# Decay tables of a gated recurrent mixer: one running sum over 128 tokens and more exponentials, in place of 16-token sums and doubling

## The chip, the cores and the metric

One core of one Trainium2 chip. The metric is device time in microseconds (us) for one execution of the whole kernel. The engines are named as the profile names them: PE is TensorE (PEld its weight loads), DVE VectorE, ACT ScalarE, POOL GpSimd, and SP issues transfers.

## The reference

A bidirectional encoder of two layers on 1024 tokens of width 1024. Layer 0 mixes with windowed attention, layer 1 with a gated linear recurrence in both directions; each also has four cross-attention heads and ends with a convolutional feed-forward. The change lies in the recurrence, one head of which is (8 heads, keys and values 128 wide, in each direction):

```python
f = lb + (1.0 - lb) * sigmoid(z)          # forget gate, per key channel
log_f, k = log(f), 1.0 - f
b = cumsum(log_f, axis=2)                 # within a chunk
q_dec = q * exp(b)
k_dec = k * exp(-b)
k_end = k * exp(b_end - b)
s = where(causal, q_dec @ k_dec.T, 0)     # o_intra = s @ v
...
o = q_dec @ state
state = exp(b_end) * state + k_end.T @ v
```

The chunk length is free: the same result follows from any cut of the tokens. What has to be right is that no exponential overflows, since `exp(-b)` grows with the length over which `b` is summed.

## The kernel before

Matrix products run on PE as three products of split operands (a high part `wh`, `uh` and a rest `wl`, `ul`): `mm3`, lines 80 to 82. ACT makes the high part (`wunit`, a cast, line 75), DVE the rest (line 76).

The mixer is `hgrn()`. `proj(h)` projects for a head: `proj_fm` makes q and the two gates' inputs with channels on the partitions, 512 tokens at a time, into one of two PSUM banks `pj`; its exponentials go to `q` and to `s`. Every second head, `proj_tm` makes v and the output gate of two heads, for 8 tiles of 128 tokens, two tiles in turn in the two `pj` banks. A bank of it is read by DVE (copy to `v`, line 1113), by ACT (first of the three activations of `sigmoid`, line 1091; the other two, lines 1092 and 1093, work on `gs`) and by DVE again (product, line 1115). There are four such passes, in what the page shows as about 1262 to 1310, 1424 to 1470, 1588 to 1634 and 1752 to 1799 us.

`direction(h, r, d, b, ...)` is called 32 times (8 heads, 2 directions, 2 halves of 512 tokens). Within a chunk of 128 tokens it builds the products of queries and keys `pa` in blocks: 32x32 blocks on the diagonal (from E2 and E1), and one level each of 32 and of 64 tokens below it (from G). Their factors need decays relative to a point near the block. Before, the sum `B` starts anew every 16 tokens (`smask`), `R` is the rest to the end of the 16, `EP` and `ER` are their exponentials, and `step(n)` doubles the length that EP and ER cover by multiplying one half of each with the other's end value (lines 1217, 1218), until they cover 128 and serve `qin`, `dec` and the keys for the state. Then four transposes of ER (line 1256), its copy `kT`, the products `pu` (line 1261), and the state's steps `S` on DVE (line 1270). `output` sums what meets the queries and normalizes it (`po`, lines 1285 and 1292; squares on line 99).

`early` is the pool of the tables: five buffers E, two EP and two ER, 2 KB each a partition. A scheduler sets the order in which each engine's queue holds its instructions, from dependencies, buffers, priorities and its own estimates; on the chip each engine runs its queue in that order. `tc.high_priority(AHEAD)` raises the instructions inside it, here the handling of the banks and the `pa` products.

Of the kernel before, what the change touches and what calls it, by code (L numbers as in the profile page):

```python
# [46 lines left out]
def build(tc, A, out):  # L47
# [983 lines left out]
    def hgrn():  # L1031
# [28 lines left out]
        nc.sync.dma_start(bng, A["b_norm_g"])  # L1060
        gm = [one([P, 512], f"gm{d}", U8) for d in range(2)]
        for d in range(2):
            gf = early.tile([P, 512], F32, tag="E", bufs=5, name="gf")
            nc.sync.dma_start(gf, A["gmask"][d])
            dve.tensor_copy(gm[d], gf)
        smask = one([P, 512], "smask", BF16)
        pool.memset(smask, 1.0)
        pool.memset(smask.rearrange("p (b c) -> p b c", c=16)[:, :, 0:1], 0.0)
        lmx = one([P, 2, 8], "lmx")
        dve.tensor_tensor(lmx, lg[:, :, 0, :], lg[:, :, 1, :], op=ALU.max)  # L1070
        dve.tensor_tensor(lg, lg, bc(lmx.unsqueeze(2), [P, 2, 2, 8]), op=ALU.subtract)
# [90 lines left out]
        def direction(h, r, d, b, qin, S, As):  # L1162

            q, k = r["q"][b], r["s"][d][b]
            rev = slice(None, None, -1) if d else slice(None)
            lt, er = (0, 1) if d else (1, 0)

            def E():
                return early.tile([P, 512], F32, tag="E", bufs=5, name="E")

            def halves(x, n):
                x = x.rearrange("p (b a c) -> p b a c", a=2, c=n)
                return x[:, :, lt, :], x[:, :, er, :]


            a_ = E()
            act.activation(k, k, AF.Ln, bias=1.0)
            act.activation(k, k, AF.Exp, scale=-1.0)
            act.activation(a_, k, AF.Ln, bias=lb[:, d, h:h + 1], scale=oml[:, d, h:h + 1])
            act.activation(k, k, AF.Identity, bias=oml[:, d, h:h + 1], scale=noml[:, d, h:h + 1])  # L1180
            R, B = E(), E()
            dve.tensor_tensor_scan(B[:, rev], smask, a_[:, rev], 0.0, op0=ALU.mult, op1=ALU.add)
            v16 = lambda x: x.rearrange("p (b c) -> p b c", c=16)
            e = 0 if d else 15
            dve.tensor_tensor(v16(R), bc(v16(B)[:, :, e:e + 1], [P, 32, 16]), v16(B), op=ALU.subtract)

            EP = early.tile([P, 512], F32, tag="EP", bufs=2, name="EP")
            ER = early.tile([P, 512], F32, tag="ER", bufs=2, name="ER")
            act.activation(EP, B, AF.Exp)
            act.activation(ER, R, AF.Exp)  # L1190
            pa = PA[d]
            E1, E2 = E(), E()
            Bl, Be = halves(B, 16)
            Rl, Re = halves(R, 16)
            l1, e1 = halves(E1, 16)
            l2, e2 = halves(E2, 16)

            def parts(n):
                return halves(EP, n) + halves(ER, n) + halves(q, n) + halves(k, n)

            pl_, pe_, rl_, re_, ql, qe, kl, ke = parts(16)
            act.activation(e1, Re, AF.Exp, scale=-1.0)
            act.activation(l2, Bl, AF.Exp, scale=-1.0)
            dve.tensor_tensor(l1, pl_, ql, op=ALU.mult)
            dve.tensor_tensor(e2, re_, ke, op=ALU.mult)
            dve.tensor_tensor(e1, e1, qe, op=ALU.mult)
            dve.tensor_tensor(l2, l2, kl, op=ALU.mult)
            def block(c, i, j, x, y, n=32):

                return pe.matmul(pa[i:i + 32, c, j:j + n], x[:, c * P + i:c * P + i + 32], y[:, c * P + j:c * P + j + n],  # L1210
                                 start=True, stop=True, tile_position=(0, i))

            def step(n):
                pl_, pe_, rl_, re_ = parts(n)[:4]
                e = 0 if d else n - 1
                nb = 512 // (2 * n)
                dve.tensor_tensor(re_, re_, bc(pl_[:, :, e:e + 1], [P, nb, n]), op=ALU.mult)
                dve.tensor_tensor(pl_, pl_, bc(pe_[:, :, e:e + 1], [P, nb, n]), op=ALU.mult)

            for n in (32, 64):  # L1220
                step(n // 2)
                G = E()
                gl, ge = halves(G, n)
                pl_, pe_, rl_, re_, ql, qe, kl, ke = parts(n)
                pool.tensor_tensor(gl, pl_, ql, op=ALU.mult)
                dve.tensor_tensor(ge, re_, ke, op=ALU.mult)
                if n == 32:
                    G32 = G
            with tc.high_priority(AHEAD):
                for c in range(4):  # L1230
                    for o in (0, 32):
                        mm = block(c, er * 64 + o, lt * 64, G, G, 64)
                with tc.issue_after(mm.ins):
                    for c in range(4):
                        for o in range(0, P, 32):
                            block(c, o, o, E2, E1)
                    for c in range(4):
                        for o in (0, 64):
                            block(c, o + er * 32, o + lt * 32, G32, G32)
            step(64)  # L1240
            dec = wp.tile([P, 4], F32, tag="dec", bufs=2, name="dec")
            e = 0 if d else P - 1
            pool.tensor_copy(dec.unsqueeze(2), EP.rearrange("p (c t) -> p c t", t=P)[:, :, e:e + 1])
            bs = slice(b * 512, (b + 1) * 512)
            sum_steps[1].send(pool.tensor_tensor(qin[:, bs], EP, q, op=ALU.mult))
            dve.tensor_tensor(ER, ER, k, op=ALU.mult)
            dve.copy_predicated(Az[d], gm[d], pa.rearrange("p c t -> p (c t)"))
            a2 = lambda x: x.rearrange("p c t -> p (c t)")
            if As[b] is None:
                As[b] = wp.tile([P, 4, P], F32, tag="As", bufs=2, name="As")  # L1250
                act.copy(a2(As[b]), Az[d])
            else:
                pool.tensor_tensor(a2(As[b]), a2(As[b]), Az[d], op=ALU.add)
            tp = bank("pt")
            for c in range(4):
                pe.transpose(tp[:, c, :], ER[:, c * P:(c + 1) * P], ident)
            kT = wp.tile([P, 4, P], F32, tag="kT", bufs=1, name="kT")
            act.copy(kT, tp)
            pu = bank("pu")
            for c in range(4):  # L1260
                pe.matmul(pu[:, c, :], kT[:, c, :], r["v"][:, 4 * b + c, :], start=True, stop=True)
            for c in (range(3, -1, -1) if d else range(4)):
                cg = 4 * b + c
                nx = cg - 1 if d else cg + 1
                if not 0 <= nx < NT:
                    continue
                if cg == (NT - 1 if d else 0):
                    act.copy(S[:, nx, :], pu[:, c, :])
                else:
                    dve.scalar_tensor_tensor(S[:, nx, :], S[:, cg, :], dec[:, c:c + 1], pu[:, c, :],  # L1270
                                             op0=ALU.mult, op1=ALU.add)
# [300 lines left out]
```

## Time and profile before

| | |
|---|---|
| median of 3 runs | 2664.08 us (2660.1 to 2664.66) |
| the profiled execution | 2660.75 us, span 2658.9 us |
| PE busy | 2605.2 us, 98% of the span |
| DVE, ACT, POOL busy | 67%, 53%, 18% |
| granted clock of PE | 0.997 |
| the mixer's stretch, 1227.6 to 1900 us | PE 662.5, DVE 476.1, ACT 377.4, POOL 179.2 of 672.4 us |

A group's row in the profile reads: line, engine, operation, written tile <- read tiles, shapes, count, then busy time in us and mean ns of one, then the idle time of the engine in front of these instructions and what ended it. The tile names are the program's; `E` stands for any of the E buffers, `s` for what the code calls `k` in `direction`.

### The profile page before, as it was taken

What the parts mean: (1) busy time and instruction counts of PE and PEld (TensorE: products, weight loads), DVE (VectorE), ACT (ScalarE), POOL (GpSimd) and SP (SyncE); (2) the same over time, 40 slices, a digit from 0 to 9 for tenths busy, and PEclk for the clock granted to TensorE, in tenths of its full rate; (3) what the DMA queues carried; (4) which work ended last, traced back from release to release, by engine and by line L of the source; (5) the groups of instructions that cost most, each with busy time, mean ns of one, the idle gap of its engine ahead of it and who ended that gap; (6) DMA issues with size and microseconds to landing.
All of it is one profiled execution on the core that took longest, in us unless ns stands there. A gap on an engine that the chain in (4) does not pass through costs nothing. (4 is left out here: it accounts for less than half of the span.)

```text
span 2658.9 us, 39054 instructions
## 1 busy us (share of the span) xinstructions
PE 2605.2 (98%) x14420; PEld 2185.9 (82%) x14420; DVE 1771.2 (67%) x2948; ACT 1399.1 (53%) x2534; POOL 472.2 (18%) x520
## 2 busy tenths in 40 slices
PE   8999999999999999999999999999999999999998
PEld 7888887788888888887888878888887788888887
DVE  6678886578555565477677675876757755656447
ACT  6467676545444445455464554656534444445453
POOL 0321010211111100032234131231211111110013
PEclk9999999999999999999999999999999999999999
DMA  9782222367777756674236251103336778785666
GB/s 353 243 176 58 74 86 83 101 193 194 198 201 195 206 154 221 215 265 151 84 112 167 66 124 54 53 25 113 127 105 195 194 193 209 198 202 170 205 207 236
DMA packets 195727, 425.92 MB, mean 160 GB/s; under 512 B 20048, under 2 KB 56272, under 8 KB 189904
## 3 DMA queue, kind: packets, MB, share of 16 engines
q1 hardware_dynamic: 161552, 324.06, 37.6%
q0 software_dynamic: 24544, 90.19, 16.3%
q10 hardware_dynamic: 9440, 9.19, 1.0%
q8 instruction: 113, 1.85, 0.3%
q14 instruction: 78, 0.64, 0.1%
HBM read 330.04 MB, written 116.39 MB: 168 GB/s over the span
## 5 line engine op out<-in xcount | busy, mean ns | idle before, releaser
L86 DVE TENSOR_TENSOR wl<-st,wh 128x1024 fp32r<-128x1024 f32 (+1 forms) x238 | 261.4, 1105 | 316.8 <-ACT wh L85 294.1
L85 ACT CAST wh<-st 128x1024 fp32r<-128x1024 f32 (+1 forms) x238 | 222.4, 937 | 288.7 <-PE X L574 186.5
L80 PE MATMUL pj<-uh,wh 128*128 128x512 f32 x512 | 203.6, 398 | 2.2 <-DVE q L1129 0.8
L574 PE MATMUL X<-wl,wh 128*128 128x512 f32 x528 | 205.0, 390 | 0.3 <-DVE wl L86 0.3
L574 PE MATMUL X<-wh,wl 128*128 128x512 f32 x528 | 204.9, 389 | 0.0
L81 PE MATMUL pj<-ul,wh 128*128 128x512 f32 x512 | 202.4, 395 | 0.0
L82 PE MATMUL pj<-uh,wl 128*128 128x512 f32 x512 | 202.3, 395 | 0.0
L574 PE MATMUL X<-wh 128*128 128x512 f32 x528 | 198.6, 390 | 0.0
L80 PE MATMUL pj<-wh,uh 128*128 128x384 f32 (+1 forms) x512 | 189.4, 372 | 5.0 <-DVE gs L1115 2.6
L82 PE MATMUL pj<-wh,ul 128*128 128x384 f32 (+1 forms) x512 | 187.7, 367 | 0.0
L81 PE MATMUL pj<-wl,uh 128*128 128x384 f32 (+1 forms) x512 | 187.2, 366 | 0.0
L76 DVE TENSOR_TENSOR wl<-st,wh 128x1024 fp32r<-128x1024 f32 (+1 forms) x91 | 113.9, 1256 | 30.9 <-ACT wh L75 29.8
L574 PE MATMUL V<-uh,wh 128*128 128x512 f32 x336 | 130.7, 389 | 0.0
L574 PE MATMUL V<-ul,wh 128*128 128x512 f32 x336 | 130.7, 389 | 0.0
L574 PE MATMUL V<-uh,wl 128*128 128x512 f32 x336 | 130.7, 389 | 0.0
L75 ACT CAST wh<-st 128x1024 fp32r<-128x1024 f32 (+1 forms) x97 | 97.8, 1014 | 37.5 <-PE pj L81 16.4
L574 PEld LDWEIGHTS X<-wl,wh 128*128 128x128 f32 x528 | 99.1, 188 | 21.6 <-DVE wl L86 1.2
L574 PEld LDWEIGHTS X<-wh,wl 128*128 128x128 f32 x528 | 99.1, 188 | 20.7
L574 PEld LDWEIGHTS X<-wh 128*128 128x128 f32 x528 | 99.1, 188 | 20.5
L80 PEld LDWEIGHTS pj<-uh,wh 128*128 128x128 f32 x512 | 96.5, 189 | 21.7 <-DVE q L1129 1.2
L82 PEld LDWEIGHTS pj<-uh,wl 128*128 128x128 f32 x512 | 96.5, 189 | 19.0
L81 PEld LDWEIGHTS pj<-ul,wh 128*128 128x128 f32 x512 | 96.5, 188 | 18.6 <-DVE ul L86 0.4
(411 smaller groups left out, 7149.2 us busy)
## 6 DMA issues: line engine op xcount, KB each, us to landing
st<-hid SPq DMA_DIRECT2D x154, 256.0 KB, 3.4
st<-in_ffw_dram SPq DMA_DIRECT2D x108, 256.0 KB, 3.7
w2s<-in_ffw_dram POOLq DMA_DIRECT2D x24, 1024.0 KB, 8.0
st<-in_ffw_dram SPq DMA_DIRECT2D x46, 512.0 KB, 4.3
hid<-tt SPq DMA_DIRECT2D x88, 256.0 KB, 4.7
st<-w2s SPq DMA_DIRECT2D x88, 256.0 KB, 3.2
sx<-in_ffw_dram SPq DMA_DIRECT2D x84, 256.0 KB, 3.9
sy<-in_ffw_dram SPq DMA_DIRECT2D x42, 512.0 KB, 6.4
```

Source lines behind the costliest of these rows:

```text
L75: act.copy(h[:, :n], raw)
L76: (eng or dve).tensor_tensor(l[:, :n], raw, h[:, :n].bitcast(F32), op=ALU.subtract)
L80: pe.matmul(o, ah, bh, start=first, stop=False)
L81: pe.matmul(o, ah, bl, start=False, stop=False)
L82: return pe.matmul(o, al, bh, start=False, stop=last)
L85: act.copy(h, src)
L86: dve.tensor_tensor(l, src, h.bitcast(F32), op=ALU.subtract)
L574: last = pe.matmul(o, x, y, start=new, stop=e, skip_group_check=not first)
```

## The change

`B` is now one sum over each chunk of 128 tokens (`smask` is zero at every 128th). For blocks of length 2n, `from_middle(n)` subtracts from B its own value at the block's middle, for n = 16, 32 and 64, each on all 512 columns on DVE. E1 and E2 are exponentials of that difference with plus and minus sign on all columns; the level factors G are exponentials of half of the columns each, written in place, and multiplied by q on POOL and by k on DVE as before. EP is one exponential of B; ER four exponentials, one for each chunk of 128, with the chunk's end value as the bias. R and the doubling steps are gone. Buffers: four E, two D (which also holds the logarithm), one B, one EP, one ER; nine in all, as before.

```diff
--- before.py
+++ after.py
@@ -1060,12 +1060,12 @@
         nc.sync.dma_start(bng, A["b_norm_g"])
         gm = [one([P, 512], f"gm{d}", U8) for d in range(2)]
         for d in range(2):
-            gf = early.tile([P, 512], F32, tag="E", bufs=5, name="gf")
+            gf = early.tile([P, 512], F32, tag="E", bufs=4, name="gf")
             nc.sync.dma_start(gf, A["gmask"][d])
             dve.tensor_copy(gm[d], gf)
         smask = one([P, 512], "smask", BF16)
         pool.memset(smask, 1.0)
-        pool.memset(smask.rearrange("p (b c) -> p b c", c=16)[:, :, 0:1], 0.0)
+        pool.memset(smask.rearrange("p (b c) -> p b c", c=P)[:, :, 0:1], 0.0)
         lmx = one([P, 2, 8], "lmx")
         dve.tensor_tensor(lmx, lg[:, :, 0, :], lg[:, :, 1, :], op=ALU.max)
         dve.tensor_tensor(lg, lg, bc(lmx.unsqueeze(2), [P, 2, 2, 8]), op=ALU.subtract)
@@ -1165,79 +1165,67 @@
             rev = slice(None, None, -1) if d else slice(None)
             lt, er = (0, 1) if d else (1, 0)
 
-            def E():
-                return early.tile([P, 512], F32, tag="E", bufs=5, name="E")
+            def E(tag="E", bufs=4):
+                return early.tile([P, 512], F32, tag=tag, bufs=bufs, name=tag)
 
             def halves(x, n):
                 x = x.rearrange("p (b a c) -> p b a c", a=2, c=n)
                 return x[:, :, lt, :], x[:, :, er, :]
 
-
-            a_ = E()
             act.activation(k, k, AF.Ln, bias=1.0)
             act.activation(k, k, AF.Exp, scale=-1.0)
+            a_ = E("D", 2)
             act.activation(a_, k, AF.Ln, bias=lb[:, d, h:h + 1], scale=oml[:, d, h:h + 1])
             act.activation(k, k, AF.Identity, bias=oml[:, d, h:h + 1], scale=noml[:, d, h:h + 1])
-            R, B = E(), E()
+            B = E("B", 1)
             dve.tensor_tensor_scan(B[:, rev], smask, a_[:, rev], 0.0, op0=ALU.mult, op1=ALU.add)
-            v16 = lambda x: x.rearrange("p (b c) -> p b c", c=16)
-            e = 0 if d else 15
-            dve.tensor_tensor(v16(R), bc(v16(B)[:, :, e:e + 1], [P, 32, 16]), v16(B), op=ALU.subtract)
-
-            EP = early.tile([P, 512], F32, tag="EP", bufs=2, name="EP")
-            ER = early.tile([P, 512], F32, tag="ER", bufs=2, name="ER")
-            act.activation(EP, B, AF.Exp)
-            act.activation(ER, R, AF.Exp)
+
+            def from_middle(n):
+
+                D = E("D", 2)
+                v = lambda x: x.rearrange("p (b c) -> p b c", c=2 * n)
+                m = n if d else n - 1
+                dve.tensor_tensor(v(D), v(B), bc(v(B)[:, :, m:m + 1], [P, 512 // (2 * n), 2 * n]), op=ALU.subtract)
+                return D
+
+            D = from_middle(16)
+            E1, E2 = E(), E()
+            act.activation(E1, D, AF.Exp)
+            act.activation(E2, D, AF.Exp, scale=-1.0)
+            dve.tensor_tensor(E1, E1, q, op=ALU.mult)
+            dve.tensor_tensor(E2, E2, k, op=ALU.mult)
             pa = PA[d]
-            E1, E2 = E(), E()
-            Bl, Be = halves(B, 16)
-            Rl, Re = halves(R, 16)
-            l1, e1 = halves(E1, 16)
-            l2, e2 = halves(E2, 16)
-
-            def parts(n):
-                return halves(EP, n) + halves(ER, n) + halves(q, n) + halves(k, n)
-
-            pl_, pe_, rl_, re_, ql, qe, kl, ke = parts(16)
-            act.activation(e1, Re, AF.Exp, scale=-1.0)
-            act.activation(l2, Bl, AF.Exp, scale=-1.0)
-            dve.tensor_tensor(l1, pl_, ql, op=ALU.mult)
-            dve.tensor_tensor(e2, re_, ke, op=ALU.mult)
-            dve.tensor_tensor(e1, e1, qe, op=ALU.mult)
-            dve.tensor_tensor(l2, l2, kl, op=ALU.mult)
             def block(c, i, j, x, y, n=32):
 
                 return pe.matmul(pa[i:i + 32, c, j:j + n], x[:, c * P + i:c * P + i + 32], y[:, c * P + j:c * P + j + n],
                                  start=True, stop=True, tile_position=(0, i))
 
-            def step(n):
-                pl_, pe_, rl_, re_ = parts(n)[:4]
-                e = 0 if d else n - 1
-                nb = 512 // (2 * n)
-                dve.tensor_tensor(re_, re_, bc(pl_[:, :, e:e + 1], [P, nb, n]), op=ALU.mult)
-                dve.tensor_tensor(pl_, pl_, bc(pe_[:, :, e:e + 1], [P, nb, n]), op=ALU.mult)
-
+            G = {}
             for n in (32, 64):
-                step(n // 2)
-                G = E()
-                gl, ge = halves(G, n)
-                pl_, pe_, rl_, re_, ql, qe, kl, ke = parts(n)
-                pool.tensor_tensor(gl, pl_, ql, op=ALU.mult)
-                dve.tensor_tensor(ge, re_, ke, op=ALU.mult)
-                if n == 32:
-                    G32 = G
+                D = from_middle(n)
+                G[n] = E()
+                (dl, de), (gl, ge), (ql, _), (_, ke) = (halves(x, n) for x in (D, G[n], q, k))
+                act.activation(gl, dl, AF.Exp)
+                act.activation(ge, de, AF.Exp, scale=-1.0)
+                pool.tensor_tensor(gl, gl, ql, op=ALU.mult)
+                dve.tensor_tensor(ge, ge, ke, op=ALU.mult)
             with tc.high_priority(AHEAD):
                 for c in range(4):
                     for o in (0, 32):
-                        mm = block(c, er * 64 + o, lt * 64, G, G, 64)
+                        mm = block(c, er * 64 + o, lt * 64, G[64], G[64], 64)
                 with tc.issue_after(mm.ins):
                     for c in range(4):
                         for o in range(0, P, 32):
                             block(c, o, o, E2, E1)
                     for c in range(4):
                         for o in (0, 64):
-                            block(c, o + er * 32, o + lt * 32, G32, G32)
-            step(64)
+                            block(c, o + er * 32, o + lt * 32, G[32], G[32])
+            EP, ER = E("EP", 1), E("ER", 1)
+            act.activation(EP, B, AF.Exp)
+            for c in range(4):
+                x = slice(c * P, (c + 1) * P)
+                m = c * P + (0 if d else P - 1)
+                act.activation(ER[:, x], B[:, x], AF.Exp, bias=B[:, m:m + 1], scale=-1.0)
             dec = wp.tile([P, 4], F32, tag="dec", bufs=2, name="dec")
             e = 0 if d else P - 1
             pool.tensor_copy(dec.unsqueeze(2), EP.rearrange("p (c t) -> p c t", t=P)[:, :, e:e + 1])
```

The set of PE's instructions is the same, and so are SP's transfers. What stands in the queues is not. The first place is ACT's queue in the third pass of `proj_tm`, where the banks of v and gate of the second and third tile are handled. Before:

```order
L1091 ACTIVATE gs<-pj 128x2x128
L1092 ACTIVATE gs<-gs 128x2x128
L1093 ACTIVATE gs<-gs 128x2x128
L1258 COPY kT<-pt 128x512
L1091 ACTIVATE gs<-pj 128x2x128
L1190 ACTIVATE ER<-E 128x512
L1092 ACTIVATE gs<-gs 128x2x128
L1093 ACTIVATE gs<-gs 128x2x128
L1179 ACTIVATE E<-s,lb,oml 128x512
L1180 ACTIVATE s<-s,oml,noml 128x512
L1091 ACTIVATE gs<-pj 128x2x128
L1092 ACTIVATE gs<-gs 128x2x128
```

After, from the third tile on (line numbers have moved below the change: 1178 and 1179 are the former 1179 and 1180, 1208 and 1209 the new exponentials of G, 1228 the pieces of ER):

```order
L1091 ACTIVATE gs<-pj 128x2x128
L1228 ACTIVATE ER<-B 128x128 x2
L1178 ACTIVATE D<-s,lb,oml 128x512
L1092 ACTIVATE gs<-gs 128x2x128
L1208 ACTIVATE E<-D 128x4x64
L1209 ACTIVATE E<-D 128x4x64
L1179 ACTIVATE s<-s,oml,noml 128x512
L1093 ACTIVATE gs<-gs 128x2x128
L1091 ACTIVATE gs<-pj 128x2x128
L1228 ACTIVATE ER<-B 128x128 x4
L1092 ACTIVATE gs<-gs 128x2x128
L1193 ACTIVATE E<-D 128x512
```

Between the first and the third activation of a tile's gate stood one exponential or nothing; now six others stand there in the third tile (two pieces of ER count as two), and eight in the fourth, of which the list shows the first four.

The second place is PE's queue in the same pass, at the end of the second pair of tiles. Before, a block of `pa` in the midst of a tile, and then transposes and products:

```order
L82 MATMUL pj<-wh,ul 128x512
L1261 MATMUL pu<-v,kT 128x128 x2
L1256 MATMUL pt<-ident,ER 128x128 x4
L80 MATMUL pj<-wh,uh 128x512
L81 MATMUL pj<-wl,uh 128x512
L1210 MATMUL pa<-E 32x64 x8
L1210 MATMUL pa<-E 32x32 x24
L82 MATMUL pj<-wh,ul 128x512
```

After, with the products of the states and the transposes of ER ahead of the block, all between two tiles:

```order
L82 MATMUL pj<-wh,ul 128x512
L1249 MATMUL pu<-v,kT 128x128
L1244 MATMUL pt<-ident,ER 128x128 x4
L1200 MATMUL pa<-E 32x64 x8
L1200 MATMUL pa<-E 32x32 x24
L80 MATMUL pj<-wh,uh 128x512
L81 MATMUL pj<-wl,uh 128x512
L82 MATMUL pj<-wh,ul 128x512
```

The block and the transposes have moved to the boundary where PE next needs a bank back.

The third place is DVE's queue in the first call of `direction`. Before:

```order
L1182 SCALAR_TENSOR_TENSOR E<-smask,E 128x512
L1185 TENSOR_TENSOR E<-E 128x512
L1204 TENSOR_TENSOR E<-EP,q 128x16x16
L1205 TENSOR_TENSOR E<-ER,s 128x16x16
L1206 TENSOR_TENSOR E<-E,q 128x16x16
L1217 TENSOR_TENSOR ER<-ER,EP 128x16x16
L1207 TENSOR_TENSOR E<-E,s 128x16x16
L1218 TENSOR_TENSOR EP<-EP 128x16x16
L1226 TENSOR_TENSOR E<-ER,s 128x8x32
```

After:

```order
L1181 SCALAR_TENSOR_TENSOR B<-smask,D 128x512
L1188 TENSOR_TENSOR D<-B 128x512 x2
L1234 TENSOR_TENSOR ER<-ER,s 128x512
L1195 TENSOR_TENSOR E<-E,q 128x512
L1196 TENSOR_TENSOR E<-E,s 128x512
L1188 TENSOR_TENSOR D<-B 128x512
L1211 TENSOR_TENSOR E<-E,s 128x8x32
```

The doubling steps and the half-width products have left, the differences and full-width products stand there, and the product for the state (`ER<-ER,s`) has moved ahead of those for `pa`.

## The prediction

> **What bounds the kernel now.** I read the page first, for the busy shares, then the stage of the change in a table of windows, then TensorE's waits in that stage, then the groups of instructions that the change touches, and last the timeline of one handover.
>
> ```profile
> span 2658.9 us, 39054 instructions
> ...
> PE 2605.2 (98%) x14420; PEld 2185.9 (82%) x14420; DVE 1771.2 (67%) x2948; ACT 1399.1 (53%) x2534; POOL 472.2 (18%) x520
> ```
>
> ```profile
> 1227.60:1900.00 672.40, 662.54 (x5233) 557.43 (x5233) 476.09 (x941) 377.37 (x801) 179.15 (x189) 1.00 0.31 90
> ```
>
> The second fence is the recurrent mixer alone (columns: window, length, busy time and count of PE, weight loads, DVE, ACT, POOL, then clock, DMA share, GB/s). TensorE is busy 662.5 of 672.4 us at full clock. The change leaves its instructions as they are, so they give nothing back; at most the 9.9 us of idle time can be won. DVE is at 71% there, ACT at 56%, POOL at 27%. So the question is which waits TensorE has now, and which it gets. In the same stretch it waits for:
>
> ```profile
> PE pj L80 <- DVE gs L1115: 2.6, 3, 1.2
> PE pu L1261 <- DVE S L1270: 2.5, 2, 1.7
> PE pt L1256 <- ACT ot L1315: 2.3, 2, 2.1
> PE pj L80 <- DVE q L1129: 0.8, 1, 0.8
> PE po L1285 <- DVE S L1270: 0.6, 1, 0.6
> ```
>
> (total, times, longest). No row names `pa`, the product that the decay tables feed: TensorE never waits for the tables, and a shorter way to them wins nothing by itself. The largest wait is another: in the four passes that project v and the gate, TensorE fills two banks in turn, and a bank is free again only after DVE's copy of v, three activations of the gate on ACT, and DVE's product. The timeline of one such handover:
>
> ```profile
> 1455.63 0.39 PE L82 MATMUL pj<-wh,ul 128*128 128x512 f32 x1
> 1455.86 0.39 PE L80 MATMUL pj<-wh,uh 128*128 128x512 f32 x1
> ...
> 1458.58 0.39 PE L80 MATMUL pj<-wh,uh 128*128 128x512 f32 x1
> ```
>
> ```profile
> 1456.06 0.43 DVE L1113 COPY v<-pj 128x256 f32<-128x256 f32 x1 [4.10 <-PE pj L82]
> 1457.84 0.42 DVE L1115 TENSOR_TENSOR gs<-pj,gs 128x256 f32<-128x256 f32 x1 [1.35 <-ACT gs L1093]
> ```
>
> ```profile
> 1456.52 0.38 ACT L1091 ACTIVATE gs<-pj 128x256 f32<-128x256 f32 x1 [5.02 <-DVE v L1113]
> 1456.94 0.42 ACT L1092 ACTIVATE gs<-gs 128x256 f32<-128x256 f32 x1
> 1457.39 0.42 ACT L1093 ACTIVATE gs<-gs 128x256 f32<-128x256 f32 x1
> ```
>
> The bank is complete at 1456.02 (1455.63 + 0.39) and free at 1458.26, 2.2 us later. Meanwhile TensorE runs the last twelve matmuls of the other bank, from 1455.86 on, and at 1458.58 it starts on the first bank again. The slack is 0.3 us. Whatever else ACT does between the first and the third of these activations beyond 0.3 us is paid by TensorE, unless it has other work there.
>
> **The change, part by part.** Durations are means in the stage:
>
> ```profile
> L1217 DVE TENSOR_TENSOR ER<-ER,EP 128x256 f32<-128x256 f32 x96 | 57.1, 595 | 2.1
> L1218 DVE TENSOR_TENSOR EP<-EP 128x256 f32<-128x256 f32 x96 | 44.2, 460 | 5.8 <-POOL E L1225 1.9
> L1246 DVE TENSOR_TENSOR ER<-ER,s 128x512 f32<-128x512 f32 x32 | 22.8, 714 | 0.1
> L1185 DVE TENSOR_TENSOR E<-E 128x512 f32<-128x512 f32 x32 | 21.9, 685 | 1.2
> L1205 DVE TENSOR_TENSOR E<-ER,s 128x256 f32<-128x256 f32 x32 | 20.6, 643 | 7.8 <-ACT ER L1190 7.4
> L1204 DVE TENSOR_TENSOR E<-EP,q 128x256 f32<-128x256 f32 x32 | 18.5, 579 | 0.2 <-ACT EP L1189 0.2
> L1206 DVE TENSOR_TENSOR E<-E,q 128x256 f32<-128x256 f32 x32 | 14.5, 452 | 1.7 <-ACT E L1202 1.7
> L1207 DVE TENSOR_TENSOR E<-E,s 128x256 f32<-128x256 f32 x32 | 13.3, 417 | 0.0
> ```
>
> DVE, for each of the 32 calls of `direction`: out go the subtraction for R (0.69), three doubling steps (3 x 1.06 = 3.17) and four half-width products (2.09), 5.94 us; in come three differences at R's price (2.06) and two full-width products at L1246's (1.43), 3.49 us. DVE loses 2.45 us a call, 78 us in all, and falls to about 59% of the stage.
>
> ```profile
> L75 ACT CAST wh<-st 128x1024 fp32r<-128x1024 f32 x44 | 46.1, 1049 | 20.2 <-PE pj L81 16.4 <-PE pj L82 3.3
> L1179 ACT ACTIVATE E<-s,lb,oml 128x512 f32<-128x512 f32 x32 | 26.1, 815 | 2.7 <-DVE oml L1080 1.8
> L1190 ACT ACTIVATE ER<-E 128x512 f32<-128x512 f32 x32 | 20.2, 632 | 1.8 <-DVE E L1185 0.6 <-PE pj L81 0.4
> L1258 ACT COPY kT<-pt 128x512 f32<-128x512 f32 x32 | 18.8, 586 | 5.6 <-PE pt L1256 5.6
> L99 ACT ACTIVATE junk<-po 128x128 bf16<-128x128 f32 x60 | 16.4, 274 | 3.0 <-PE po L1285 1.9
> L223 ACT ACTIVATE xp<-ps,nm 128x256 f32<-128x256 f32 x32 | 14.8, 475 | 33.5 <-PE pu L1261 17.5 <-DVE nm L220 16.0
> L1202 ACT ACTIVATE E<-E 128x256 f32<-128x256 f32 x32 | 13.0, 407 | 0.0
> L1251 ACT COPY As<-Az 128x512 f32<-128x512 f32 x16 | 9.8, 614 | 4.1 <-PE po L1285 4.1
> L1315 ACT ACTIVATE ot<-pt,bng 128x512 f32<-128x512 f32 x14 | 9.5, 679 | 2.9 <-DMA oT<-ot 2.3 <-DMA oT<-xo 0.6
> ```
>
> ACT: out go ER in one piece (0.63) and two half exponentials (0.81); in come E1 and E2 (2 x 0.63), four half exponentials for the levels 32 and 64 (4 x 0.41) and ER in four 128-wide pieces with a bias of their own. No row shows such a piece: below it stand the 128-wide square (0.27), above it the 256-wide exponential with a bias (0.48). From 256 to 512 elements an exponential grows by 0.225 us, so 128 would take 0.30 without a bias; two operands read per partition make L1179 0.18 longer than L1190, so one adds 0.09: I take 0.40, near the middle. The balance is +1.26 +1.63 +1.60 -1.44 = 3.05 us a call (2.5 to 3.4 at the ends for ER), 98 us in all. ACT comes to 475 of 672 us, 71%: no new bound as a mean.
>
> POOL keeps its instructions and sizes; its factor is now ACT's exponential and no longer DVE's doubled table. SP and all DMAs are as before; the mask's memset (32 columns to 4) happens once. EP and ER shrink from two buffers to one, so EP's exponential waits for POOL's `qin` of the call before; what queues behind it on ACT are weight casts and bank copies. POOL is 27% busy and EP stands late in its call, so I cost this at nothing; without that cover it is a rival below. The same holds for the single B, whose scan on DVE now waits for the exponentials of the call before (behind it stand the copies of v), and for four E instead of five, where E1 waits for `pa` of the call before: a call has 672 / 32 = 21 us of the stage.
>
> Where the price falls is in the order, shown with the change: ready exponentials now stand inside the gate's triples. In the order before, seven triples hold foreign instructions; with the rows above these are 1.63, 1.25, 0.59, 0.63, 1.05 (a weight cast), 0.63 and 0.59 us, together 6.4, and the trace has 2.6 us of waiting there in three places: 41% comes through, the rest goes into the slack or beside other work of TensorE. In the order after, twelve triples do: in the first pass 1.6, 3.9 and 0.6 us, in the second 2.9, 4.0 and 2.9, in the third and fourth 1.6 (four pieces of ER), 3.2 (two pieces, two half exponentials, and the two of L1179's price) and 3.7 (four pieces, E1, E2, two half exponentials) each, together 33.0. At 41% that is 13.5 us. From below: in the third and fourth passes TensorE has four transposes to do behind the first of these triples, and a block of `pa` and four transposes behind the second:
>
> ```profile
> 1397.38 1.17 PE L1210 MATMUL pa<-E 128*32 128x64 f32 x64
> 1398.48 0.66 PE L1256 MATMUL pt<-ident,ER 128*128 128x128 f32 x4
> ```
>
> so 1.6 - 0.3 - 0.7 = 0.6 and 3.2 - 0.3 - 1.8 = 1.1 us reach it, with the third triple between nothing (ACT caught up during the waits) and 3.4; four such passes give 7 to 20 us. I take 11, between this lower end and the calibrated value, and subtract the 2.6 that are there now: +8.4 us. The other waits I leave where they are: of the 3.1 us for S some may go with DVE's load, and the attention units between (whose casts wait behind the same exponentials) may add as much.
>
> The Trainium skill has a rule on this price: "ScalarE: Activation LUTs", section "What ACT_TABLE_LOAD costs", gives an activation with one pointer operand 280 ns + 0.833 ns an element, thus an estimate of 0.39 us for a piece, and says that successive activations overlap by about 93 ns. The trace agrees on the second: the successor of a 0.40 us activation starts 0.30 us after it.
>
> ```profile
> 1442.13 0.40 ACT L1202 ACTIVATE E<-E 128x256 f32<-128x256 f32 x1
> 1442.43 0.40 ACT L1203 ACTIVATE E<-E 128x256 f32<-128x256 f32 x1
> ```
>  By that rule the 67 foreign instructions of the order after cost 6.2 us less than 33.0 and the nine of before 0.8 less than 6.4, so that 26.8 x 2.6 / 5.6 = 12.4 stands for 13.5; the sum would lose 1 us.
>
> The sum: 2660.75 us for the profiled execution (span 2658.9 and 1.85 around it) + 8.4 = 2669.2. The median of the runs shown, 2664.08, is 3.3 above that execution, so the forecast is 2672 us, 0.3% slower. The measurement can tell about 0.2%, 5.3 us, from no change.
>
> **The rivals.** *Faster: DVE's relief.* The waits above in which DVE comes last sum to 6.5 us. If the triples' foreign work hid in TensorE's own and all these vanished, the median would be 2657.6, 0.24% faster. For it: DVE was the laggard of the chain, and it loses 78 us. Against: it decides only if less than 0.3 us of ACT's work stood in each triple, and the order has 0.6 us in one and 1.6 to 4 in eleven. The Trainium skill's "SBUF — State Buffer", "Who interferes with whom", would strengthen it: a DVE instruction with two SBUF inputs locks out GpSimd's reads, and 192 doubling steps leave; but the new differences also have two inputs. 0.10.
>
> *No change: the lag is absorbed.* ACT idles between the passes' triples:
>
> ```profile
> sum 187.00, PE 184.26 PEld 152.54 DVE 126.87 ACT 83.90 POOL 53.03; mean PE 46.06 PEld 38.13 DVE 31.72 ACT 20.98 POOL 13.26
> ```
>
> (the four passes: ACT 84 of 187 us). If a wait in one triple lets ACT catch up for the next, only the 7 us from below come through, 4.4 net, and DVE's relief may take back part or all of it: 2664 to 2668. 0.27.
>
> *Much slower: ACT blocked.* If EP with its single buffer, or the four pieces of ER that wait for the transposes of the call before, held ACT for 1 us in each of 32 calls, with bank copies behind it, up to 32 us would come on top: 2680 to 2704. For it: everything on ACT runs in order. Against: the waits of POOL are long only where TensorE sets the pace. 0.13.
>
> **How the numbers follow.** My forecast, the triples' waits alone, has 0.50 and reaches from 2668 to 2682; below 5.3 us of loss it counts as no change, about 0.02 of it. Slower is thus 0.48 + 0.13 = 0.61, no change 0.29, faster 0.10. The range 2659 to 2688 leaves out the faster case nearly whole and the upper half of the blocked one, under 2 in 10.
>
> **What would show it.** Right: PE busy in the stage unchanged, its idle time near 18 us, the row `PE pj <- DVE gs` grown from 2.6 to 8 to 16 us over some ten waits, ACT's third activation of the gate late in the second to fourth tile of a pass; DVE in the stage near 398 us, ACT near 475; an ER piece near 0.40 us. Wrong: that row below 5 us (the lag is absorbed), or waits of TensorE for `pt`, `pa` or `pu` behind ACT that exceed it (the blocked case).

## The result, and the profile after

The changed kernel takes 2677.62 us (median of 6 runs, 2676.01 to 2683.99); the kernel before 2663.61 us (median of 6). The ratio on record is 1.0065, 95% interval 1.0055 to 1.0075: 0.65% slower. (The two medians alone differ by 14.0 us, 0.53%.) The profiled execution took 2682.89 us, 5.3 above its median; against the profile of before that is 22.1 us more. All times here and below are of executions at the usual granted clock; one execution of e2, the profiled one, ran at 0.276 of it for 9219.6 us, so e2's median is of its three others and its sums are missing.

The mixer's stretch of the kernel after, which now ends 20 us later (columns as in the prediction: window, length, busy time and count of PE, weight loads, DVE, ACT, POOL, then clock, DMA share, GB/s):

```profile
1227.60:1920.00 692.40, 673.77 (x5235) 567.80 (x5236) 443.72 (x739) 447.91 (x1019) 178.88 (x188) 0.98 0.31 87
```

DVE fell by 32 us and ACT rose by 71. TensorE's clock is 0.98 where it was 1.00. What TensorE waits for in the stage after the change (total, times, longest):

```profile
PE pt L1244 <- DVE ER L1234: 9.1, 3, 3.0
PE pb L80 <- ACT s L1134: 4.0, 1, 4.0
PE pa L1200 <- DVE E L1211: 2.2, 2, 1.8
PE pj L80 <- ACT s L1134: 1.7, 1, 1.7
PE pu L1249 <- DVE v L1113: 1.1, 1, 1.1
```

The row `PE pj <- DVE gs`, on which the forecast stood, is gone. Instead three equal waits of 3.04 us stand in heads 1, 3 and 5, where the keys' table ER is turned. The first of them on TensorE (start, duration, what it did, in brackets the idle time before and what ended it):

```profile
1392.15 0.39 PE L82 MATMUL pj<-uh,wl 128*128 128x512 f32 x1
1395.58 0.66 PE L1244 MATMUL pt<-ident,ER 128*128 128x128 f32 x4 [3.04 <-DVE ER L1234]
...
1398.09 0.63 PE L82 MATMUL pj<-uh,wl 128*128 128x512 f32 x1
...
1400.40 0.39 PE L82 MATMUL pj<-uh,wl 128*128 128x512 f32 x1
```

After the wait the same matmul takes 0.63 instead of 0.39 us, then 0.39 again. The windows show why (same columns as the first fence):

```profile
1390.00:1395.00 5.00, 2.54 (x15) 1.83 (x13) 4.87 (x9) 4.14 (x11) 2.42 (x4) 1.00 0.84 269
1395.00:1400.00 5.00, 4.42 (x19) 3.84 (x20) 4.46 (x7) 4.51 (x12) 1.79 (x2) 0.67 0.69 257
...
1560.00:1565.00 5.00, 3.57 (x15) 3.38 (x16) 4.96 (x10) 4.50 (x12) 1.80 (x2) 0.55 0.60 115
1565.00:1570.00 5.00, 5.00 (x32) 3.80 (x34) 1.35 (x4) 3.29 (x8) 2.34 (x3) 0.77 0.20 26
```

Each of the three waits has a stretch at half clock at its end or just behind it, 3.4 us long (1396.7 to 1400.1) or 6.8 (1560.5 to 1567.3, the second pair of windows), which costs half its length where TensorE is working. I summed both for the stage, from 137 windows of 5 us between 1230 and 1915 us: TensorE's idle time, and 5 us times the missing share of the clock. Before: 9.7 us idle and 1.7 of clock. After: 18.5 and 13.5. The sum grows by 20.6 us, but it counts some time twice: half clock while TensorE is idle costs nothing. With windows of 0.2 us and busy time alone, the clock costs 1.6 us before and 11.6 after. So of the 22.1 us between the two profiles 8.8 are idle time and 10.0 are clock, about half. In a median run the clock's part is smaller: the whole execution's mean clock was 0.992 in this one and 0.991 in the longest (2683.99 us), but 0.994 to 0.996 in the four of 2676 to 2678 us.

ACT and DVE ahead of the first of these waits:

```profile
1388.12 0.63 ACT L1224 ACTIVATE EP<-B 128x512 f32<-128x512 f32 x1 [1.01 <-DVE B L1181]
1390.86 0.63 ACT L1193 ACTIVATE E<-D 128x512 f32<-128x512 f32 x1 [2.11 <-DVE D L1188]
...
1393.15 1.28 ACT L1228 ACTIVATE ER<-B 128x128 f32<-128x128 f32 x4
```

```profile
1386.20 0.69 DVE L1234 TENSOR_TENSOR ER<-ER,s 128x512 f32<-128x512 f32 x1 [4.12 <-ACT ER L1228]
1386.81 1.22 DVE L1181 TENSOR_TENSOR_SCAN B<-smask,D 128x512 f32<-128x512 bf16 x1
...
1389.06 2.37 DVE L1188 TENSOR_TENSOR D<-B 128x512 f32<-128x512 f32 x2
...
1392.74 1.21 DVE L1188 TENSOR_TENSOR D<-B 128x512 f32<-128x512 f32 x1
...
1394.84 0.69 DVE L1234 TENSOR_TENSOR ER<-ER,s 128x512 f32<-128x512 f32 x1
```

ACT stands 2.11 us for a difference, with the four pieces of ER queued behind it. Two differences take 2.37 us here; at other places two take 1.29 (at 1341.80, for one). POOL at the same time:

```profile
1388.83 1.45 POOL L1233 TENSOR_TENSOR qin<-EP,q 128x512 f32<-128x512 f32 x1 [9.33 <-ACT EP L1224]
...
1392.40 1.00 POOL L1210 TENSOR_TENSOR E<-E,q 128x256 f32<-128x256 f32 x1 [0.97 <-ACT E L1208]
```

All the slow differences run beside a product of POOL, the pair beside the one for `qin`, the single one beside one for a factor G. The stage as a whole shows the same: of its 96 differences 65 take under 0.70 us, and each of the other 31, up to 1.79 us, overlaps a product or sum of POOL. The groups of the stage say the same in the mean (busy us, mean ns | idle before):

```profile
L1188 DVE TENSOR_TENSOR D<-B 128x512 f32<-128x512 f32 x96 | 84.9, 905 | 0.6
L1211 DVE TENSOR_TENSOR E<-E,s 128x256 f32<-128x256 f32 x64 | 37.2, 584 | 3.1 <-ACT E L1209 3.1
L1195 DVE TENSOR_TENSOR E<-E,q 128x512 f32<-128x512 f32 x32 | 27.5, 858 | 4.4 <-ACT E L1193 3.6
L1196 DVE TENSOR_TENSOR E<-E,s 128x512 f32<-128x512 f32 x32 | 25.8, 806 | 0.0
L1210 POOL TENSOR_TENSOR E<-E,q 128x256 f32<-128x256 f32 x64 | 66.6, 1041 | 141.7 <-ACT E L1208 120.8 <-issue 17.5 <-PE po L1273 3.2
L1228 ACT ACTIVATE ER<-B 128x128 f32<-128x128 f32 x128 | 41.2, 394 | 5.5 <-DVE v L1113 2.7 <-DVE B L1181 1.5 <-PE pt L1244 1.2
```

### The profile page after: what moved, and what is told of

Read it like the earlier page. It is cut to its first block, busy times and chain, and to the rows that moved or that the text cites. A ratio compares the mean times of both kernels' runs of the same rounds, so it can differ in the third digit from the quotient of the medians.

```text
span 2681.1 us, 39054 instructions
## 1 busy us (share of the span) xinstructions
PE 2616.2 (98%) x14420; PEld 2196.3 (82%) x14420; DVE 1741.0 (65%) x2756; ACT 1467.7 (55%) x2758; POOL 474.6 (18%) x520
## 5 line engine op out<-in xcount | busy, mean ns | idle before, releaser
L574 PEld LDWEIGHTS X<-wh,wl 128*128 128x128 f32 x528 | 99.1, 188 | 20.6
L75 ACT CAST wh<-st 128x1024 fp32r<-128x1024 f32 (+1 forms) x97 | 97.7, 1013 | 27.7 <-PE pj L82 10.0
```

Source lines behind the costliest of these rows:

```text
L75: act.copy(h[:, :n], raw)
L574: last = pe.matmul(o, x, y, start=new, stop=e, skip_group_check=not first)
```

## The experiments

Five theories were tried. **A**: a single buffer of ER puts its pieces behind the transposes of the call before. **B**: ACT's load. **C**: nothing systematic, each new order of the scheduler loses something. **D**: DVE's operations, stretched beside POOL's, and what stands behind them. **E**, a later form of A: the calls bunch. The experiments ran on several chips, each beside the kernel before, which took 2660.5 to 2661.6 us there; so the ratio is what compares best between rows. The last three columns are the two sums from 5 us windows of the profiled execution, as above, and their total; the clock's column holds up to 2 us of half clock in idle time, which cost nothing.

| run | median us | ratio to before, 95% interval | idle | clock | sum |
|---|---|---|---|---|---|
| before | 2663.61 | | 9.7 | 1.7 | 11.4 |
| after | 2677.62 | 1.0065 (1.0055 to 1.0075) | 18.5 | 13.5 | 32.0 |
| e1 EP in place | 2684.73 | 1.0087 (1.0073 to 1.0100) | 26.1 | 8.5 | 34.6 |
| e2 two ER | 2689.44 | 1.0108 (1.0093 to 1.0124) | | | |
| e3 before, few buffers | 2669.44 | 1.0026 (1.0015 to 1.0037) | 14.3 | 3.5 | 17.8 |
| e4 ER in one piece | 2689.25 | 1.0103 (1.0086 to 1.0121) | 24.9 | 10.2 | 35.1 |
| e5 before, exponentials doubled | 2666.97 | 1.0021 (1.0013 to 1.0030) | 13.9 | 3.4 | 17.3 |
| e6 after, no level exponentials | 2682.25 | 1.0070 (1.0057 to 1.0084) | 24.3 | 8.6 | 32.9 |
| e7 after, no POOL products | 2666.89 | 1.0014 (1.0005 to 1.0023) | 14.0 | 1.7 | 15.7 |
| e8 before, other turn | 2669.22 | 1.0029 (1.0018 to 1.0040) | 15.8 | 3.4 | 19.2 |
| e9 tables in place | 2681.97 | 1.0077 (1.0064 to 1.0091) | 21.4 | 13.8 | 35.2 |
| e10 products on DVE | 2667.80 | 1.0024 (1.0015 to 1.0033) | 14.5 | 3.4 | 17.9 |
| e11 both remedies | 2668.10 | 1.0027 (1.0016 to 1.0037) | 13.3 | 6.8 | 20.1 |
| e12 before, products on DVE | 2662.25 | 1.0002 (0.9993 to 1.0011) | 7.4 | 1.7 | 9.1 |

In every profile the execution's own time minus the last column gives 2648 to 2652 us. So what separates these executions is, to about 4 us, TensorE's waits in this stage and the half clock near them. That says where the time goes, not yet why.

### Buffers and the pieces of ER: e1 to e4

**e1**, the control for e2:

```diff
-            EP, ER = E("EP", 1), E("ER", 1)
+            bs = slice(b * 512, (b + 1) * 512)
+            EP, ER = qin[:, bs], E("ER", 1)
...
-            sum_steps[1].send(pool.tensor_tensor(qin[:, bs], EP, q, op=ALU.mult))
+            sum_steps[1].send(pool.tensor_tensor(EP, EP, q, op=ALU.mult))
```

> The changed kernel, with EP's exponential written straight into its half of qin and multiplied by q there on POOL, so that the buffer EP is gone; B and ER keep one buffer each. It is the control for the next kernel. Theory A (one buffer for ER: the four pieces of ER stand on ACT behind the transposes of the call before, and TensorE waits for ER with its clock halved afterwards): the waits of PE pt for DVE ER stay, 9 us in all, and the time stays at 2672 to 2683 us. Theory B (ACT's load, 70 us more of exponentials in the stage, wherever they stand): 2675 to 2680. Theory C (nothing systematic: every new order loses some other 5 to 20 us): any time from 2664 to 2690, with the waits at other places.

Measured 1.0087, and the waits moved. Of the 9.1 us for ER 1.5 are left; these come instead:

```profile
PE pa L1200 <- DVE E L1211: 8.7, 4, 2.9
PE pu L1249 <- DVE S L1258: 6.8, 2, 3.5
PE pj L80 <- DVE gs L1115: 4.0, 4, 1.4
```

A's range and B's are both missed. The places of the waits aren't fixed, but in each of these three rows DVE is what TensorE waited for. The three equal waits are thus a symptom of this one order.

**e2**: the same with `E("ER", 2)`.

> As the kernel with EP in place, but ER has two buffers (the room that EP left). Theory A: the three waits of 3.04 us for ER go, and with them the stretches at half clock behind them (3.4, 6.8 and 3.4 us in the trace, which cost half of that): 9.1 + 6.8 = 16 us less than the changed kernel, 2662 us (2657 to 2668). If waits alone counted and the clock were an accident, 9 us less: 2669. Theory B: ACT's load is the same, 2675 to 2680. Theory C: as far from the changed kernel as the control is, in either direction.

Theory A fails: with the second buffer the time is 2689.44, not 2662.

**e3**: the kernel before with `bufs=4` for E and 1 for EP and ER.

> The kernel before with the buffers of the changed one: four E, one EP, one ER (in place of five, two, two), its 16-token sums and its doubling untouched. Theory A: one ER is what costs, and here it is held longer, through the doubling: slower than before by 5 to 20 us (2669 to 2684), with PE pt waiting for DVE ER. Theory B: ACT has the work of before, so the time of before, 2664 +- 4 us. Theory C: cannot say, any of these.

0.26% slower, at the lower edge of what A gave, but the waits for ER are 0.7 us of 14; TensorE's waits spread over eleven rows, 2.1 us at most each. By itself that told buffers and chance apart no better than e8 does below.

**e4**:

```diff
-            for c in range(4):
-                x = slice(c * P, (c + 1) * P)
-                m = c * P + (0 if d else P - 1)
-                act.activation(ER[:, x], B[:, x], AF.Exp, bias=B[:, m:m + 1], scale=-1.0)
+            v = lambda x: x.rearrange("p (c t) -> p c t", t=P)
+            m = 0 if d else P - 1
+            dve.tensor_tensor(v(ER), bc(v(B)[:, :, m:m + 1], [P, 4, P]), v(B), op=ALU.subtract)
+            act.activation(ER, ER, AF.Exp)
```

> The changed kernel with ER from one difference on DVE (end value minus B, full width) and one exponential on ACT, in place of four pieces with a bias: ACT's 1.28 us becomes 0.63, DVE gets some 0.9. ER still has one buffer. Theory A: the difference itself must wait for the buffer, so ER comes no earlier: waits of PE pt for ER stay within 6 to 12 us, time 2672 to 2683. Theory B: ACT loses 21 us of its 70 us surplus, so about a third of the loss goes: 2673. Theory C: any time from 2664 to 2690.

Less on ACT and more on DVE: 1.0103, slower than the changed kernel itself, whose interval ends at 1.0075. B said 2673; A's range ends at 2683, and the waits for ER are 3.9 us, below its 6 to 12; only C's range holds. That the time grew with work moved from ACT to DVE was a first hint at DVE, no more, since the order is new here too.

### Which engine's work it is: e5 to e8

**e5**: the activations of EP and ER in the kernel before written twice, those of `e1` and `l2` three times.

> The kernel before, with superfluous exponentials that write the same values again: EP and ER twice, the two halves of 256 for the 16-token level three times each, about 2.9 us more on ACT in each of the 32 calls (93 us, near the changed kernel's surplus), nothing more on DVE or POOL. Theory B (the exponentials themselves, by load and by length of the chain on ACT): slower than before by as much as the change, 2672 to 2685 us. Theory D (DVE: its differences are stretched while POOL reads, 0.68 us alone and 1.78 beside a product of POOL, and its in-order queue is late with what TensorE waits for): ACT has room, 2659 to 2668. Theory C (each new order loses something, no cause in the work): as the neutral kernel of this batch.

From 1227 to 1915 us:

```profile
1227.00:1915.00 688.00, 674.08 (x5273) 566.72 (x5273) 469.53 (x944) 443.52 (x996) 172.56 (x189) 1.00 0.31 89
```

ACT is busy 443.5 us, as in the changed kernel (443.9 in this window, 386.7 before). It costs 0.21%, a third of the change's 0.65% and no more than e8 loses by order alone.

**e6**:

```diff
-                act.activation(gl, dl, AF.Exp)
-                act.activation(ge, de, AF.Exp, scale=-1.0)
-                pool.tensor_tensor(gl, gl, ql, op=ALU.mult)
-                dve.tensor_tensor(ge, ge, ke, op=ALU.mult)
+                pool.tensor_tensor(gl, dl, ql, op=ALU.mult)
+                dve.tensor_tensor(ge, de, ke, op=ALU.mult)
```

> The changed kernel without the four exponentials of the levels 32 and 64 (the factors G are made from the differences themselves, so the output isn't the reference's): ACT loses 1.6 us a call, 51 us in all, and the chain to G is shorter by an activation; DVE and POOL keep every instruction. Theory B: half or more of the loss goes, 2662 to 2669 us. Theory D: DVE is late as before, 2673 to 2684. Theory C: 2664 to 2690.

```profile
1227.00:1915.00 688.00, 663.31 (x5197) 558.38 (x5198) 446.09 (x738) 406.91 (x885) 178.35 (x188) 0.99 0.29 85
```

ACT loses 37 us in this window and nothing is won: 1.0070. So more load on ACT costs little (e5), less gains nothing (e6): B fails from both sides.

**e7**: the line `pool.tensor_tensor(gl, gl, ql, op=ALU.mult)` left out.

> The changed kernel without POOL's two products of the factors G with q a call (so the output isn't the reference's): POOL loses 64 instructions, and DVE's differences have less beside them. Theory D: the mean of the differences falls from 0.905 to below 0.8 us, DVE loses 10 to 25 us in the stage, and most of the loss goes, 2662 to 2669 us. Theory B: ACT is as it was, 2673 to 2684. Theory C: 2664 to 2690.

Ratio 1.0014; the median is 10.7 us below the changed kernel's. DVE is busy 425.0 us from 1227 to 1915 us, against 439.7. The two groups of DVE beside which POOL now has less to do:

```profile
L1188 DVE TENSOR_TENSOR D<-B 128x512 f32<-128x512 f32 x96 | 70.0, 752 | 0.6
L1210 DVE TENSOR_TENSOR E<-E,s 128x256 f32<-128x256 f32 x64 | 27.5, 431 | 4.0 <-ACT E L1209 4.0
```

A difference falls from 905 to 752 ns, the product with k from 584 to 431, with not one instruction of DVE changed. As theory D gave it. But the kernel leaves out more than a neighbour of DVE: the products were also a step on the way to G, 1.04 us long on POOL.

**e8**:

```diff
-            for i, (d, b) in enumerate(((0, 0), (1, 1), (0, 1), (1, 0))):
+            for i, (d, b) in enumerate(((1, 1), (0, 0), (0, 1), (1, 0))):
```

> The kernel before with nothing but the first two of a head's four calls of direction exchanged: the same instructions, sizes and buffers, in an order that the scheduler makes anew. Theory C: a new order alone loses as the changed kernel does, 2668 to 2690 us, with waits of TensorE at places of their own and stretches at half clock behind those over 2 us. Theories B and D: the work is that of before, 2659 to 2668.

1.0029: the same work in a new order costs about 7.7 us. Theory C is right to this size: one new order alone moved the time by 0.3%. It doesn't reach the 0.65 to 1.08% of the changed kernel and its variants with POOL's products.

### Bunching, and POOL's products: e9 to e12

The profile showed one more thing of the single ER. In head 1 the scans of the four calls start at 1340.5, 1356.6, 1386.8 and 1395.7 us; before, at 1334.6, 1354.0, 1365.9 and 1387.3. The reading was that the third call waits for the transposes of the second, and the fourth treads on its heels.

**e9**: E1 and the two G made in their differences, EP in `qin`; five E, two B, two ER.

```diff
-            E1, E2 = E(), E()
-            act.activation(E1, D, AF.Exp)
-            act.activation(E2, D, AF.Exp, scale=-1.0)
+            E1, E2 = D, E()
+            act.activation(E2, D, AF.Exp, scale=-1.0)
+            act.activation(E1, D, AF.Exp)
...
-                G[n] = E()
+                G[n] = D
```

> The changed kernel with the same arithmetic in fewer tables: E1 and the two G are made in place in their differences, EP in qin, and the room goes to a second buffer of B and of ER (five E, two B, two ER; nine in all). Theory E (bunching: with one ER the third call of a head waits for the transposes of the second; its scan starts 30 us after the second's and the fourth follows within 9 us, where the kernel before has 20, 12 and 21 us between them; in the bunch DVE, ACT and POOL can't follow TensorE): the third scan comes within 20 us of the second, and the time is 2660 to 2669 us. Theory D (DVE's operations stretched beside POOL's, wherever the calls stand): 2673 to 2690, since every instruction stays.

The bunch is gone (two scans of DVE in head 1, the second and third of its calls):

```profile
1363.36 1.23 DVE L1181 TENSOR_TENSOR_SCAN B<-smask,E 128x512 f32<-128x512 bf16 x1 [0.76 <-ACT E L1178]
1375.45 1.23 DVE L1181 TENSOR_TENSOR_SCAN B<-smask,E 128x512 f32<-128x512 bf16 x1
```

and the time stays: 1.0077. Theory E fails.

**e10**:

```diff
-                pool.tensor_tensor(gl, gl, ql, op=ALU.mult)
+                dve.tensor_tensor(gl, gl, ql, op=ALU.mult)
```

> The changed kernel with POOL's two products of the factors G with q moved to DVE (64 of 0.41 us, 26 us more there; POOL loses 67 us). Theory D: DVE's differences fall below 0.8 us in the mean, so DVE's total in the stage stays within 15 us of the changed kernel's 444, a link through POOL leaves the chain, and the time is 2662 to 2672 us. Theory E: one ER and the bunch remain, and DVE has 26 us more to do: 2676 to 2695.

```profile
L1188 DVE TENSOR_TENSOR D<-B 128x512 f32<-128x512 f32 x96 | 71.9, 773 | 0.5
L1210 DVE TENSOR_TENSOR E<-E,q 128x256 f32<-128x256 f32 x64 | 27.7, 433 | 1.1 <-ACT E L1208 1.0
L1211 DVE TENSOR_TENSOR E<-E,s 128x256 f32<-128x256 f32 x64 | 27.5, 430 | 0.0
```

```profile
1227.00:1915.00 688.00, 673.51 (x5267) 566.29 (x5266) 446.08 (x816) 447.83 (x1026) 119.44 (x124) 1.00 0.31 90
```

DVE does 64 products more, 27.7 us, and its busy time is 446.1 against 439.7 us of the changed kernel in the same window: it had lost nearly as much standing beside POOL. The same work as the changed kernel's, with a median 9.8 us lower and intervals that don't touch (1.0015 to 1.0033, 1.0055 to 1.0075). Of the 9.1 us for ER 3.9 are left, one wait of 3.1 among them.

**e11**: e9 and e10 together.

> Tables in place with two buffers of B and of ER, and POOL's products of the factors G on DVE: both remedies, all of the arithmetic kept. If both act, the waits for POOL and DVE go and the third call comes early: 2658 to 2665 us, level with the kernel before or better. If only the products count (theory D): 2664 to 2672, as with the products alone. If the buffers do harm by the order that they bring, as the tables in place did by themselves: 2672 to 2685.

2668.1 us: 13.9 less than e9, no better than e10. The buffers bring nothing in either pair.

**e12**: the same move of the products in the kernel before.

> The kernel before with POOL's two products of G with q a call on DVE: the control for the same move in the changed kernel. If work of POOL beside DVE is dear whatever the scheme, TensorE's 10 us of waits in the stage shrink: 2652 to 2659 us. If the kernel before hides it, since its doubled tables reach POOL early and nothing of the chain returns from ACT: 2659 to 2668, and DVE, already the busiest beside TensorE, grows by less than 26 us. If DVE is too full for it: above 2668.

```profile
1227.00:1915.00 688.00, 680.52 (x5317) 572.13 (x5316) 479.15 (x1018) 387.41 (x819) 120.00 (x126) 1.00 0.31 91
```

No difference (1.0002), with 9.1 us of waits and clock left. Here, too, DVE takes on 64 products without growing (485.9 before the move), but TensorE was hardly waiting for it.

No version is faster than the kernel before.

## Why the prediction came out as it did

The direction was right and the time lay within the range, but the term that gave the number did not occur. By its steps:

**The bound.** Right that TensorE sets the time and had 9.9 us of idle time to win. Its idle time, forecast as "near 18 us", was measured as 18.5; that this agrees is luck, since the waits that were summed are not those measured. Its busy time, forecast as unchanged, rose from 662.5 to 673.8 us, by the half clock.

**ACT and the pieces of ER.** A piece is 0.394 us, as the 0.40 taken. ACT's rise was put too high, 98 us against 71 (448 us, not 475): pieces in a row overlap, and four of them take 1.28 us, not 1.6. e5 and e6 show that this load costs little.

**The gate's triples, 11 us.** This is the step that failed: the waits for `gs`, forecast at 11 us and given as "wrong" below 5, went from 2.6 us to nothing. The triples did grow. One in the second pass:

```profile
1453.78 0.38 ACT L1091 ACTIVATE gs<-pj 128x256 f32<-128x256 f32 x1 [0.87 <-DVE v L1113]
1454.06 0.69 ACT L1228 ACTIVATE ER<-B 128x128 f32<-128x128 f32 x2
...
1456.61 0.40 ACT L1093 ACTIVATE gs<-gs 128x256 f32<-128x256 f32 x1
```

DVE's product came at 1459.08. But TensorE ran 24 matmuls of projection from 1453.70 on, and a block for `pu` behind them, and went on at 1459.64 without a wait. The slack of 0.3 us was read from one handover of the old order, where twelve matmuls lay between; the new order had put more there. Neither that slack nor the 41% that came through before could be carried over to an order in which TensorE's queue had changed as well. In other orders of the changed kernel the row returns, with 4.0 (e1), 3.2 (e4) and 5.1 us (e9), never with the 8 to 16 forecast.

**DVE, minus 78 us.** Mis-sized: it fell by 32. The differences were priced at 685 ns, the mean of L1185 and also what a difference takes undisturbed, and took 905; the full-width products, priced at 714, took 858 and 806. The prices were means of other instructions, with other neighbours on POOL.

**"POOL keeps its instructions and sizes", at no cost.** The second failed step, and what the runs put in place of the first. The 64 products stayed, but now start with the ends of ACT's exponentials, beside DVE's differences and its product with k: the latter is 584 ns on DVE where the same product before the change was

```profile
L1226 DVE TENSOR_TENSOR E<-ER,s 128x256 f32<-128x256 f32 x64 | 28.4, 443 | 0.0
```

Taking these products from POOL (e7, e10, and e11 against e9) gives back 10 to 14 us; each of the three changed kernels without them is faster than each of the six with them, 2666.9 to 2668.1 against 2677.6 to 2689.4 us. The Trainium skill, "SBUF — State Buffer", section "Who interferes with whom", has the rule: a DVE instruction with two SBUF inputs contends with a GpSimd instruction that reads SBUF. The trace agrees, with 0.68 us for a difference alone and 1.79 beside POOL's sum `As`. The prediction named the rule, but as help for the faster rival, since doubling steps leave; the three differences and two full-width products that come in have two SBUF inputs as well.

**The clock.** Not in the sum at all: in the profiled execution it cost 11.6 us against 1.6, a rise as large as that of the idle time.

**The rivals.** "ACT blocked" described the three places for ER best: an engine in order, one buffer, pieces behind others' waits; its sign, waits for `pt` that exceed those for `gs`, came. Its time, 2680 to 2704, was too high, and its cause wrong: two buffers of ER don't help (e2, e9). "The lag is absorbed" was right about the triples, but not about the time, 2664 to 2668. That the measured 2677.6 us lies within the forecast's own 2668 to 2682 is luck.

**What stays open.** Why the products cost so much is shown in part. e7, e10 and e11 remove them both as DVE's neighbours and as a link to G that is slower on POOL (1.04 us) than on DVE (0.43), and no run separates the two. For the first speaks that no wait of TensorE in the changed kernel names POOL; in e6 and e9 rows of 2.8 and 3.4 us for POOL's E do. Nor was the changed kernel itself merely reordered: that 10 to 14 us are more than an order is worth rests on e8 and on the nine times that don't overlap. With the products on DVE the changed kernel is 0.24% slower than before. e3, e5 and e8, variants of the kernel before in other orders, lose 0.21 to 0.29%, so no cause in the work can be read from it. Nor did a run show why POOL's products cost the kernel before nothing (e12). What differs is that before each level followed from DVE's own doubling, now from an exponential between two visits to DVE: from the start of a scan to the end of DVE's last product for G in the call I find 8.4 us in the median before and 10.6 after, 9.8 in e10 and 9.4 in e7 (with POOL's products 9.3 before and 10.6 after). e6 shortens this way to 8.1 us and is not faster; so its length alone isn't the reason.

## What to carry to other kernels

Price an instruction of DVE by what will run on POOL beside it, not by the mean of a like one elsewhere: work that moved to POOL to relieve DVE may take back the same time. Slack between an engine and its banks belongs to one order; when a change moves both queues, read the new order of the waiting engine too before counting a wait. Where the edit makes the scheduler write a new order, run a neutral reordering of the old kernel as well: here one alone moved 0.3%.

## What the runs showed of the hardware that was not expected

Short waits of TensorE cost more than themselves. In the kernel before, a wait of 2.12 us for `pt` is followed by half clock from 1542.7 to 1546.1 us; in the changed kernel the three waits of 3.04 us go with 3.4, 6.8 and 3.4 us. In e12 a wait of 0.9 and one of 1.1 us, with 0.5 us of work between, were enough for 3.4 us. So 1.7 or 3.4 us of full-speed work (once, in e9, 5.1) are lost on top, and not with each wait: one of 1.72 us that ended at 1249.5 in the changed kernel had no such stretch.

The length of a single wait doesn't decide it. Within each of the thirteen profiles every stretch begins on one grid of 3.413 us; the five in the changed kernel's stage begin 37, 48, 49 and 44 steps apart. What goes with a stretch is how busy TensorE was in the step ahead of it. In the mixer's stage of these profiles all 28 full-clock steps in which it was busy 43% or less were followed by half clock, of the eight with 46 to 50% three, and of those with more only one (58%, in e3). The two waits of e12 fall into one step, busy 41%; the wait of 1.72 us left its step 50% busy.

The Trainium skill, "TensorE: Matmul & The Clock Gate", Part 1, "What's actually happening", describes a free-running window of about 3.4 us and a clock that is either half or full; the trace agrees with both (0.50 or 1.00, one grid of 3.413 us). The same page of the Trainium skill, "Why this matters for your kernels", advises to avoid idle gaps of more than about 3 us. That is too generous here: the 2.12 us of the kernel before were enough.

The second surprise is how much order alone is worth. In thirteen profiles of much the same work TensorE's idle time and the clock add up to between 9 and 35 us in this stage, and they account for the differences in time to about 4 us.
